# w_out handed over in chunk order, keys and bias in fewer loads, another order for the last pair's products, and seeded banks at the end

## The chip, the core and the metric

The kernel runs on one core of a Trainium2 chip. The core has a matmul engine (PE, with its weight loads shown as PEld), a vector engine (DVE), a scalar engine (ACT), GpSimd (POOL) and a queue engine (SP) that issues most of the DMAs; 16 DMA engines move the data. The metric is the device time of one execution in microseconds (us), the median of several runs.

## The reference

One trunk layer is run for two batches with the same weights: a prompt of 512 tokens and a sample of 1024 tokens, width 1024, in fp32. Attention has 8 heads of 64 in 2 key/value groups and sees a window of 128 to either side; beside it runs a convolution branch.

```python
h = rmsnorm(x, norm_attn_g)
z = h @ w_in                                   # q | k | v | ca | cb
a = window_attention(q, k, v, bias, sink)      # 512 columns
c = silu(layernorm(dwconv31(ca * sigmoid(cb)))) # 512 columns
x = x + concat(a, c) @ w_out
h = rmsnorm(x, norm_ffn_g)
u = dwconv3(h @ w_up)                          # 2 x 2816 columns
x = x + (silu(u[:, :2816]) * u[:, 2816:]) @ w_down
y = rmsnorm(x, norm_final_g)
```

## The kernel before, in words

Every fp32 operand is split into a high part (a cast to fp32r, ACT, L153) and a low part (the difference, DVE or POOL, L154), and each product is three passes on PE: high x high, high x low, low x high. A pass is a matmul of 128x128 by 128x512 that writes a PSUM bank of 128x512 fp32.

The stages are: the input projection of both batches, with the convolution branch and the attention of the prompt beside it (to about 283 us); the prompt's w_out product (about 288 to 345 us), beside which the attention of the sample begins; the prompt's feed-forward (to about 790 us) with the rest of the sample's attention beside it; the sample's w_out product (780 to 900 us); and the sample's feed-forward. There the up products are computed by a scheme of seven products in place of eight for each of 22 steps (`first` to `seventh`), the last of which is step 21, the last pair; the down products use the same scheme, product after product in the order 1, 2, 5, 6, 7, 4, 3, each over 11 pairs p, each on four token blocks tt (`mm_down`, L1468).

The parts that the change touches are these.

- **w_out of the prompt.** `prompt_out` walks two halves n of the 1024 output columns. `load_wo` (L746) loads the eight chunks kc of 128 rows; chunks 0 to 3 hold the attention's rows, whose two head groups lie apart in w_out, so each takes two loads of 64 rows (L753), and chunks 4 to 7 take one each (L755). `split_wo` splits them (L153, L154), and `out_half` runs the 24 matmuls of a token block (L727, L728, L729), then adds x on DVE.
- **Keys of the sample.** The projection wrote the split keys to a DRAM tensor `ksd` of 64 rows. `load_kv` (L759) loads them into four tiles of 128 rows x 1024, one for each of two head groups and of high and low (q9, q6, q7, q1 in the program's buffer numbers), with the same 64 rows in either half of the partitions: two loads of 64 rows a tile, 4096 B a row (L765). The score matmuls of the sample (`scores`, L583) read these tiles. `attention` of the sample is interleaved with `out_half`.
- **Bias.** `load_bias` (L508) loads the band bias of each head from a DRAM tensor `bbd`, one load a head (L513).
- **The last pair.** The loop over j calls the products by hand. In the last round the first down step (`down_step(0)`) stands between `seventh` and `fourth`. A product may need a value that another engine puts into its bank: `seventh` needs the copy of `sixth` (u2, L1243), `third` the sum that `y_sum` forms (L1266).
- **The end.** `finish` (L1525) forms the mean square of a row block from two halves, takes its power on POOL, scales on ACT and DVE and stores with SP. For the blocks 2 and 3, the last, the kernel first sums product 3 in a PSUM bank, adds it on DVE to the sum o12 (L1036), and squares that (L1530).

In the stretches around the change the order of the instructions on PE (in the feed-forward on PE and SP) is that in which the code is written, while the other engines, and PE outside those stretches, are ordered by a scheduler that simulates the program. SP's DMAs take turns on eight semaphores, so that at most eight are under way; the ninth waits for the first. Tiles come from a list of named slots (q, c, h, d, s for SBUF; a, u, b, c, w for PSUM); who takes a slot again waits until its last reader is done.

Of the kernel before, what the change touches and what calls it, by code (L numbers as in the profile page):

```python
# [9 lines left out]
F32 = mybir.dt.float32  # L10
# [89 lines left out]
def tile_hybrid_encoder(ctx: ExitStack, tc: tile.TileContext, xs, rel_bias, norm_attn_g, w_in,  # L100
# [70 lines left out]
    def want_w(i):  # L171
        if i < nch and i not in ws:
            want_raw(i)
            ws[i] = split(raws.pop(i))

    class Halves:
        def __init__(self, parts):
            self.parts = parts
# [567 lines left out]

    def load_wo(kc, n):
        raw = wor[kc, n] = sb.tile([NT])
        s = slice(n * NT, (n + 1) * NT)
        if kc < 4:  # L750
            for kv in range(NKV):
                r0 = (kv * GRP + kc) * HD
                nc.sync.dma_start(raw[kv * HD:(kv + 1) * HD, :], w_out[0, r0:r0 + HD, s])  # L753
        else:
            nc.sync.dma_start(raw[:], w_out[0, kc * P:(kc + 1) * P, s])  # L755

    def split_wo(kc, n, dve=False):
        wo[kc, n] = split(wor.pop((kc, n)), dve)

    def load_kv():  # L760
        for kv in range(NKV):
            kt[1, kv] = [sb.tile([1024], F32R) for _ in range(2)]
            for L in range(2):
                for half in range(2):
                    nc.sync.dma_start(kt[1, kv][L][half * HD:(half + 1) * HD, :].bitcast(F32), ksd[:, kv, L, :])  # L765
# [351 lines left out]
    class Part:  # L1117
        def __init__(self, held, n):
            self.held, self.n = held, n

        def __getitem__(self, i):
            return self.held[:, self.n, :][i]
# [98 lines left out]
    def pair_banks(j):  # L1221
        st[j] = dict(x=wide(), wy=wide())

    def armed(out):

        hi, lo = A[1, 0]
        nc.tensor.matmul(out, hi[:, 0:P], hi[:], start=True, stop=True)

    def first(j):
# [235 lines left out]
    LEAD = 4  # L1465
    CAP = 48

    def mm_down(out, i, p, tt):  # L1468
        (sh, sl), (th, tl) = hl[i, p]
        c = slice(tt * P, (tt + 1) * P)  # L1470
        nc.tensor.matmul(out, sh[:, c], th[:], start=(p == 0), stop=False)  # L1471
        nc.tensor.matmul(out, sh[:, c], tl[:], start=False, stop=False)  # L1472
        nc.tensor.matmul(out, sl[:, c], th[:], start=False, stop=(p == NPAIR - 1))  # L1473

    pair2 = lambda: [sb.tile([W2]) for _ in range(2)]
    xd = {}
# [38 lines left out]

    early = {}

    def left_first(tt):

        ss, o = early[tt] = sm(2), sb.tile([D])  # L1520
        part = cut(o11, tt)
        nc.scalar.activation(o[:, L], part, AF.Square, accum_out=ss[:, 0:1])
        nc.vector.tensor_tensor(part, part, fins[0][:, L], op=ALU.mult)

    def finish(blk, parts, tail):  # L1525
        ss, o = early.pop(blk) if tail else (sm(2), sb.tile([D]))
        rs = sm(2)
        for n in range(1 if tail else 0, 2):
            s = slice(n * NT, (n + 1) * NT)
            nc.scalar.activation(o[:, s], parts[n], AF.Square, accum_out=ss[:, n:n + 1])  # L1530
        nc.gpsimd.tensor_scalar(rs[:, 0:1], ss[:, 0:1], 1.0 / D, EPS, op0=ALU.mult, op1=ALU.add)
        nc.gpsimd.tensor_scalar(rs[:, 1:2], ss[:, 1:2], 1.0 / D, rs[:, 0:1], op0=ALU.mult, op1=ALU.add)  # L1532
        nc.gpsimd.tensor_tensor(rs[:, 1:2], rs[:, 1:2], nhalf[:, 0:1], op=ALU.pow)
        for n in range(2):
            s = slice(n * NT, (n + 1) * NT)
            if n == 0 and not tail:
                nc.scalar.activation(o[:, s], parts[n], AF.Identity, scale=rs[:, 1:2])
                nc.gpsimd.tensor_tensor(o[:, s], o[:, s], fins[0][:, s], op=ALU.mult)
            elif n == 0:
                nc.scalar.activation(o[:, s], parts[n], AF.Identity, scale=rs[:, 1:2])  # L1540
            else:
                nc.vector.scalar_tensor_tensor(o[:, s], parts[n], rs[:, 1:2], fins[0][:, s], op0=ALU.mult, op1=ALU.mult)  # L1542
            nc.sync.dma_start(GR[1]["o"][blk * P:(blk + 1) * P, s], o[:, s])

    made = 0

# [9 lines left out]
    def down_step(k):  # L1556
        i, p = steps[k]
        load_next(8 if k == 0 else 3 if len(pr) < CAP else 0)
        make(k + (LEAD if k else 1))
        if p == 0:  # L1560
            pd.extend(wide() for _ in range(2))
        for tt in range(4):
            mm_down(pd[tt // 2][:, (tt % 2) * NT:(tt % 2 + 1) * NT], i, p, tt)
        hl.pop((i, p))
        if p == NPAIR - 1:
            evacuate(i, pd)
            pd.clear()
# [12 lines left out]
        if i == 4 and p == 8:  # L1580
            with_x("o12", 0, 1)
            load_x1(1, 0)

    for j in range(2, NJ):
        for half in range(2):
            load_up(j + 3, half)
        if j >= NJ - 3:
            sb.free.extend(raws.free)
            raws.free.clear()
        if j >= NJ - 2:  # L1590
            load_next(4)
# [20 lines left out]
        third(j)  # L1612
        split_up(j + 1, 3)
    sb.free.extend(raws.free)
    value_part(NJ - 1)
# [4 lines left out]
    u, e, o11, o12 = (acc.pop(n) for n in ("u", "e", "o11", "o12"))  # L1620
    cut = lambda t, tt: t[tt // 2][:, (tt % 2) * NT:(tt % 2 + 1) * NT]
    base = len(steps) - NPAIR
    z = wide()
# [45 lines left out]

def _laid_out(np, v):  # L1670
    cols = lambda a: a.reshape(-1, P).T
    w_in = v["w_in"][0]
    cb, ca = (w_in[:, c:c + P].reshape(KC, P, P) for c in (COL_CB, COL_CA))
    laid = dict(
        xpT=v["x_prompt"][0].T.reshape(KC, P, NT),
        xsT=v["x_sample"][0].reshape(2, NT, KC, P).transpose(0, 2, 3, 1),
        w_in=_columns(w_in),
        w_up=_columns(v["w_up"][0]),
        w_first=np.concatenate([cb, ca], axis=2),
        vecs=np.concatenate([cols(v[n]) for n in ("norm_attn_g", "norm_ffn_g", "conv_dw_b", "conv_ln_g", "conv_ln_b", "ffn_dw_b")], axis=1),  # L1680
        cvw=cols(v["conv_dw_w"]),
        fw=cols(v["ffn_dw_w"]),
    )
    return {n: np.ascontiguousarray(a) for n, a in laid.items()}
# [27 lines left out]
```

## Time and profile before

| what | us |
|---|---|
| median of 3 runs | 1525.64 (1525.16 to 1525.9) |
| the profiled execution | 1529.8 |
| its span in the profile | 1528.0 |
| PE busy | 1492.7 (98% of the span) |
| DVE, ACT, POOL busy | 1177.5, 801.6, 742.9 |
| mean granted clock of PE | 0.995 |

A row of the list of waits names the engine, the tile and line that waited, whom it waited for, the us in total, how many times, and the longest. A row of the time line gives the start, the us, the engine, the line, the operation, the tiles (out<-in), and in brackets the idle time before it with what ended it. DMA rows on SPq show the issuing alone; the data land some us later, and the DMA view gives the median from issue to landing.

### The profile page before, as it was taken

The numbers are of one execution on the slowest core, as the hardware profiler recorded it, in microseconds if no ns is written. First come the engines' busy times: TensorE is split into PE (matmuls) and PEld (weight loads), VectorE is DVE, ScalarE is ACT, GpSimd is POOL, SyncE is SP. The second block draws the span as 40 slices with busy tenths as digits, with TensorE's granted clock in tenths as the row PEclk, the third lists the DMA queues.
The fourth block names the chain that finished last, engine by engine and source line by source line (L and its number), as shares of the span: only waits on it lengthen the run. The fifth ranks groups of instructions, "written<-read, shape, count | busy, mean of one in ns | idle before, by whom it ended". The sixth has DMA issues, their size and how long they took to land. (4 is left out here: it accounts for less than half of the span.)

```text
span 1528.0 us, 20034 instructions
## 1 busy us (share of the span) xinstructions
PE 1492.7 (98%) x6800; PEld 1226.7 (80%) x6800; DVE 1177.5 (77%) x1669; ACT 801.6 (52%) x1414; POOL 742.9 (49%) x648
## 2 busy tenths in 40 slices
PE   8999999899999999999999999999999999999997
PEld 7888777787888877878878888888888888788886
DVE  7877847558799989995575878888888877886794
ACT  6424454467566565665355365444444445454364
POOL 3454353228677777786542325555555554000236
PEclk9999999999999999999999999999999999999999
DMA  9455231834333333345474213333333323585642
GB/s 376 154 165 150 85 104 35 254 112 124 97 111 100 123 102 109 102 128 173 141 243 140 83 56 104 103 104 103 104 104 104 103 90 127 207 341 167 205 145 110
DMA packets 106754, 209.71 MB, mean 137 GB/s; under 512 B 11507, under 2 KB 31091, under 8 KB 106524
## 3 DMA queue, kind: packets, MB, share of 16 engines
q1 hardware_dynamic: 105404, 207.36, 41.0%
q8 instruction: 53, 0.87, 0.2%
q10 hardware_dynamic: 1248, 1.09, 0.2%
q14 instruction: 49, 0.40, 0.1%
HBM read 161.98 MB, written 47.46 MB: 137 GB/s over the span
## 5 line engine op out<-in xcount | busy, mean ns | idle before, releaser
L1039 POOL TENSOR_TENSOR q<-q,q 128x512 fp32r<-128x512 f32 x82 | 114.4, 1407 | 155.8 <-ACT q L1148 151.9
L154 POOL TENSOR_TENSOR q<-q,q 128x1024 fp32r<-128x1024 f32 x66 | 159.9, 2425 | 58.2 <-ACT q L153 21.2
L281 PE MATMUL u<-h,q 128*128 128x512 f32 x384 | 151.8, 395 | 1.3 <-DVE h L890 0.9
L282 PE MATMUL u<-h,q 128*128 128x512 f32 x384 | 150.5, 392 | 0.0
L283 PE MATMUL u<-h,q 128*128 128x512 f32 x384 | 150.2, 391 | 0.0
L1162 PE MATMUL w<-h,q 128*128 128x512 f32 x372 | 146.3, 393 | 2.4 <-ACT h L1243 1.5
L1164 PE MATMUL w<-h,q 128*128 128x512 f32 x372 | 144.9, 390 | 0.7 <-POOL q L1039 0.7
L322 DVE SCALAR_TENSOR_TENSOR c<-c,cvw,c 128x512 f32<-128x512 f32 x184 | 137.4, 747 | 1.7
L1163 PE MATMUL w<-h,q 128*128 128x512 f32 x350 | 136.3, 389 | 0.0
L1036 POOL TENSOR_TENSOR q<-q,q 128x1024 f32<-128x1024 f32 x8 | 23.9, 3001 | 180.8 <-DVE q L1036 169.4
L153 ACT CAST q<-q 128x1024 fp32r<-128x1024 f32 x66 | 69.1, 1050 | 67.6 <-POOL q L154 39.8
L1471 PE MATMUL w<-h,h 128*128 128x512 f32 x264 | 102.7, 389 | 0.0
L1473 PE MATMUL w<-h,h 128*128 128x512 f32 x264 | 102.7, 389 | 0.0
L1039 DVE TENSOR_TENSOR h<-h,h 128x512 fp32r<-128x512 f32 (+1 forms) x128 | 92.2, 762 | 11.1 <-ACT h L1043 9.0
L1039 POOL TENSOR_TENSOR c<-q,c 128x512 fp32r<-128x512 f32 x46 | 72.1, 1580 | 49.8 <-ACT c L1148 49.8
L1472 PE MATMUL w<-h,h 128*128 128x512 f32 x244 | 95.0, 390 | 0.0
L314 POOL TENSOR_TENSOR h<-h,h 128x512 f32<-128x512 f32 x57 | 76.1, 1335 | 28.4 <-ACT h L313 23.5
L1043 ACT CAST h<-h 128x512 fp32r<-128x512 f32 x101 | 58.7, 619 | 58.0 <-DVE h L1039 30.5
L1162 PEld LDWEIGHTS w<-h,q 128*128 128x128 f32 x372 | 69.8, 188 | 20.6 <-ACT w L1234 3.6
L281 PEld LDWEIGHTS u<-h,q 128*128 128x128 f32 x384 | 72.1, 188 | 16.9 <-DVE h L890 2.1
L154 POOL TENSOR_TENSOR h<-h,h 128x512 fp32r<-128x512 f32 x52 | 70.4, 1360 | 29.2 <-ACT h L153 19.7
L283 PEld LDWEIGHTS u<-h,q 128*128 128x128 f32 x384 | 72.1, 188 | 15.0 <-POOL q L154 0.4
(445 smaller groups left out, 4364.7 us busy)
## 6 DMA issues: line engine op xcount, KB each, us to landing
q<-in_laid_w_up SPq DMA_DIRECT2D x88, 512.0 KB, 3.6
h<-in_w_down SPq DMA_DIRECT2D x90, 256.0 KB, 3.6
ga<-q SPq DMA_DIRECT2D x64, 256.0 KB, 2.0
h<-ga SPq DMA_DIRECT2D x57, 256.0 KB, 3.9
q<-in_laid_w_in SPq DMA_DIRECT2D x22, 512.0 KB, 3.9
q<-in_x_sample SPq DMA_DIRECT2D x15, 512.0 KB, 6.0
h<-qsd SPq DMA_DIRECT2D x24, 256.0 KB, 3.3
qsd<-h SPq DMA_DIRECT2D x44, 128.0 KB, 2.4
```

The lines of the kernel that those rows point to most:

```text
L154: (nc.vector if dve else nc.gpsimd).tensor_tensor(lo[:], raw[:], hi[:].bitcast(F32), op=ALU.subtract)
L281: nc.tensor.matmul(out, whi[:, kc, :], hi[:], start=(kc == 0), stop=False)
L282: nc.tensor.matmul(out, whi[:, kc, :], lo[:], start=False, stop=False)
L283: nc.tensor.matmul(out, wlo[:, kc, :], hi[:], start=False, stop=(kc == KC - 1))
L322: nc.vector.scalar_tensor_tensor(acc[:], src(t), w(t), acc[:], op0=ALU.mult, op1=ALU.add)
L1039: (eng or nc.vector).tensor_tensor(out, a, b, op=ALU.subtract)
L1162: nc.tensor.matmul(out, whi[:, s], hi[:], start=(start and c == 0), stop=False, **go)
L1163: nc.tensor.matmul(out, whi[:, s], lo[:], start=False, stop=False, **go)
L1164: nc.tensor.matmul(out, wlo[:, s], hi[:], start=False, stop=(stop and c == 3), **go)
L1471: nc.tensor.matmul(out, sh[:, c], th[:], start=(p == 0), stop=False)
L1472: nc.tensor.matmul(out, sh[:, c], tl[:], start=False, stop=False)
L1473: nc.tensor.matmul(out, sl[:, c], th[:], start=False, stop=(p == NPAIR - 1))
```

## The change

w_out is handed over as a tensor in the order chunk by chunk, so that every chunk is one load of 128 rows. The two loads of a key tile become one, whose source repeats the 64 rows with a step of stride 0 in front. The bias loads of the heads that share a tile become one. In the last pair the call of `fourth` and `third` moves ahead of `seventh`, and `seventh` goes behind the first down step. At the end the banks for the last two blocks are armed and filled with o12 by ACT ahead of time, product 3 accumulates on top, and the square reads the bank; eps enters earlier, as a column of that bank, and the last block's two stores go out on ACT's and SP's queue.

```diff
     def load_bias(n):
...
-            for e in range(n):
-                nc.sync.dma_start(bt[:, e, :], bass.AP(b0.tensor, b0.offset + (h + e) * NT + P - 1, [[NH * NT - 1, P], [1, 3 * P]]))
-                bias.append((bt, e))
+            nc.sync.dma_start(bt[:], bass.AP(b0.tensor, b0.offset + h * NT + P - 1, [[NH * NT - 1, P], [NT, n], [1, 3 * P]]))
+            bias.extend((bt, e) for e in range(n))
...
     def load_wo(kc, n):
         raw = wor[kc, n] = sb.tile([NT])
-        s = slice(n * NT, (n + 1) * NT)
-        if kc < 4:
-            for kv in range(NKV):
-                r0 = (kv * GRP + kc) * HD
-                nc.sync.dma_start(raw[kv * HD:(kv + 1) * HD, :], w_out[0, r0:r0 + HD, s])
-        else:
-            nc.sync.dma_start(raw[:], w_out[0, kc * P:(kc + 1) * P, s])
+        nc.sync.dma_start(raw[:], laid["w_out"][n, :, kc, :])
...
             for L in range(2):
-                for half in range(2):
-                    nc.sync.dma_start(kt[1, kv][L][half * HD:(half + 1) * HD, :].bitcast(F32), ksd[:, kv, L, :])
+                k = ksd[:, kv, L, :]
+                nc.sync.dma_start(kt[1, kv][L][:].bitcast(F32), bass.AP(k.tensor, k.offset, [[0, 2]] + list(k.ap)))
...
-    def mm_down(out, i, p, tt):
+    def mm_down(out, i, p, tt, seeded=False):
...
-        nc.tensor.matmul(out, sh[:, c], th[:], start=(p == 0), stop=False)
+        go = dict(skip_group_check=seeded)
+        nc.tensor.matmul(out, sh[:, c], th[:], start=(p == 0 and not seeded), stop=False, **go)
...
+        if tail:
+            nc.scalar.activation(o[:, NT:D + 1], parts[2], AF.Square, accum_out=ss[:, 1:2])
+        else:
...
-        nc.gpsimd.tensor_scalar(rs[:, 0:1], ss[:, 0:1], 1.0 / D, EPS, op0=ALU.mult, op1=ALU.add)
-        nc.gpsimd.tensor_scalar(rs[:, 1:2], ss[:, 1:2], 1.0 / D, rs[:, 0:1], op0=ALU.mult, op1=ALU.add)
-        nc.gpsimd.tensor_tensor(rs[:, 1:2], rs[:, 1:2], nhalf[:, 0:1], op=ALU.pow)
...
+        nc.gpsimd.tensor_tensor(rs[:], ss[:, 1:2], nhalf[:, 0:1], op=ALU.pow)
...
-            nc.sync.dma_start(GR[1]["o"][blk * P:(blk + 1) * P, s], o[:, s])
+            (nc.scalar if n == 0 and tail else nc.sync).dma_start(GR[1]["o"][blk * P:(blk + 1) * P, s], o[:, s])
...
+            nc.scalar.activation(fins[0][:], fins[0][:], AF.Identity, scale=D ** 0.5)
...
+        last = j == NJ - 1
         value_part(j - 1)
+        if last:
+            fourth(j, None, True)
+            third(j)
         first(j + 1)
         split_up(j + 1, 6)
-        seventh(j)
-        if j == NJ - 1:
+        seventh(j, None, not last)
+        if last:
...
-        fourth(j)
+        if last:
+            y_sum(j)
+        else:
+            fourth(j)
...
+        if p == 4:
+            for tt in (2, 3):
+                zs.append(wide())
+                armed(zs[-1][:, L], hl[3, p][0][0])
+                nc.scalar.copy(zs[-1][:, L], cut(o12, tt))
...
     for tt in (2, 3):
-        left_first(tt)
-        z = wide()
+        z = zs.pop(0)
+        left_first(tt, z)
         for p in range(NPAIR):
-            mm_down(z[:, L], 3, p, tt)
-        add(cut(o12, tt), z[:, L], cut(o12, tt))
-        finish(tt, (cut(o11, tt), cut(o12, tt)), True)
+            mm_down(z[:, L], 3, p, tt, True)
+        finish(tt, (cut(o11, tt), z[:, L], z[:, 0:NT + 1]), True)
```

Line numbers shift by 7 to 27 in the changed kernel: the score matmuls are L589 there, w_out's L733 to L735, the products' L1164 to L1166, the down products' L1474 to L1476.

On SP, in the prompt's w_out product, this stood before (q6, q7 and q1 are key tiles; h58, h29, h57, h56 take w_out chunks and values; q0, q13, q2 rows of x):

```order
L769 DMA h29_438_2761<-vsd_156 128x512
L755 DMA h57_492_3031<-in_w_out 128x512
L755 DMA h56_493_3033<-in_w_out 128x512
L765 DMA q6_432_2745<-ksd_157 64x1024 x2
L765 DMA q7_433_2750<-ksd_157 64x1024 x2
L765 DMA q1_434_2751<-ksd_157 64x1024 x2
L142 DMA q0_472_2883<-in_x_prompt 128x1024
L142 DMA q13_478_2927<-in_x_prompt 128x1024
L142 DMA q2_482_2979<-in_x_prompt 128x1024
L753 DMA h18_487_3018<-in_w_out 64x512 x2
L753 DMA h6_481_2976<-in_w_out 64x512 x2
```

And this stands there now:

```order
L755 DMA h56_493_3017<-in_laid_w_out 128x512
L778 DMA h29_438_2753<-vsd_156 128x512
L774 DMA q6_432_2741<-ksd_157 128x1x1024
L774 DMA q7_433_2744<-ksd_157 128x1x1024
L774 DMA q1_434_2745<-ksd_157 128x1x1024
L142 DMA q0_472_2871<-in_x_prompt 128x1024
L142 DMA q13_478_2915<-in_x_prompt 128x1024
L755 DMA h18_487_3005<-in_laid_w_out 128x512
L142 DMA q2_482_2966<-in_x_prompt 128x1024
L755 DMA h6_481_2964<-in_laid_w_out 128x512
```

Six key loads of 64 rows became three of 128, at the same place, ahead of the same rows of x and the last two chunks of w_out. The fourth key tile, q9, is loaded ahead of all the w_out chunks, before as now.

On PE, at the end of the second token block's w_out product (bank u1) and the start of the third's (u0), the score matmuls of the sample stood so before (banks a0, a1, a2):

```order
L727 MATMUL u1_134_2929<-h12_467_2830,h34_407_2575 128x512
L728 MATMUL u1_134_2929<-h11_468_2831,h34_407_2575 128x512
L729 MATMUL u1_134_2929<-h12_467_2830,h16_408_2576 128x512
L583 MATMUL a0_130_2861<-q9_431_2744,h39_459_2808 128x256
L583 MATMUL a0_130_2861<-q6_432_2745,h39_459_2808 128x256
L583 MATMUL a1_132_2908<-q7_433_2750,h0_460_2810 128x256
L583 MATMUL a1_132_2908<-q1_434_2751,h0_460_2810 128x256
L583 MATMUL a2_133_2914<-q7_433_2750,h0_460_2810 128x256
L583 MATMUL a2_133_2914<-q1_434_2751,h0_460_2810 128x256
L727 MATMUL u0_137_2981<-h52_447_2784,h17_396_2505 128x512
```

And so now:

```order
L733 MATMUL u1_134_2917<-h12_467_2818,h34_407_2571 128x512
L734 MATMUL u1_134_2917<-h11_468_2819,h34_407_2571 128x512
L589 MATMUL a0_130_2849<-q9_431_2740,h39_459_2796 128x256
L589 MATMUL a0_130_2849<-q6_432_2741,h39_459_2796 128x256
L589 MATMUL a1_132_2896<-q7_433_2744,h0_460_2798 128x256
L589 MATMUL a1_132_2896<-q1_434_2745,h0_460_2798 128x256
L735 MATMUL u1_134_2917<-h12_467_2818,h16_408_2572 128x512
L733 MATMUL u0_137_2968<-h52_447_2772,h17_396_2501 128x512
L734 MATMUL u0_137_2968<-h51_448_2773,h17_396_2501 128x512
L589 MATMUL a2_133_2902<-q7_433_2744,h0_460_2798 128x256
L589 MATMUL a2_133_2902<-q1_434_2745,h0_460_2798 128x256
```

The first score matmuls on q7 and q1 stand one matmul earlier, ahead of the last pass of the second block.

On PE, in the last pair, behind `sixth` (bank w_44, right operand q_1756) came the first down step (w_45) and then `seventh` (q_1758), before:

```order
L1164 MATMUL w_44_11786<-h_1441_8783,q_1756_11800 128x512
L1471 MATMUL w_45_11975<-h_1783_11963,h_1781_11959 128x512
L1472 MATMUL w_45_11975<-h_1784_11964,h_1781_11959 128x512
L1473 MATMUL w_45_11975<-h_1783_11963,h_1782_11960 128x512
L1471 MATMUL w_45_11975<-h_1783_11963,h_1781_11959 128x512
L1472 MATMUL w_45_11975<-h_1784_11964,h_1781_11959 128x512
L1473 MATMUL w_45_11975<-h_1783_11963,h_1782_11960 128x512
L1162 MATMUL w_44_11786<-h_1443_8795,q_1758_11831 128x512
```

Now `fourth` (w_43, q_1761) follows `sixth` at once, and `seventh` stands between two passes of the fifth down step:

```order
L1166 MATMUL w_44_11762<-h_1441_8759,q_1756_11776 128x512
L1164 MATMUL w_43_11761<-h_1427_8684,q_1761_11828 128x512
L1165 MATMUL w_43_11761<-h_1428_8685,q_1761_11828 128x512
L1166 MATMUL w_43_11761<-h_1427_8684,q_1761_11828 128x512
L1164 MATMUL w_43_11761<-h_1429_8696,q_1761_11828 128x512
```

```order
L1474 MATMUL w_45_11977<-h_1807_12041,h_1805_12037 128x512
L1475 MATMUL w_45_11977<-h_1808_12042,h_1805_12037 128x512
L1164 MATMUL w_44_11762<-h_1443_8771,q_1758_11807 128x512
L1165 MATMUL w_44_11762<-h_1444_8772,q_1758_11807 128x512
L1166 MATMUL w_44_11762<-h_1443_8771,q_1758_11807 128x512
```

`third` stands between, behind the first half of the first down step.

More of the change, by code (lines that the diff above doesn't have):

```diff
@@ L174, in want_w, with __init__, __getitem__ @@
             ws[i] = split(raws.pop(i))
+    class Part:
+        def __init__(self, held, n):
+            self.held, self.n = held, n
+        def __getitem__(self, i):
+            return self.held[:, self.n, :][i]
     class Halves:
@@ L748, in load_wo, with load_wo_pair @@
         raw = wor[kc, n] = sb.tile([NT])
-        s = slice(n * NT, (n + 1) * NT)
-        if kc < 4:
-            for kv in range(NKV):
-                r0 = (kv * GRP + kc) * HD
-                nc.sync.dma_start(raw[kv * HD:(kv + 1) * HD, :], w_out[0, r0:r0 + HD, s])
-        else:
-            nc.sync.dma_start(raw[:], w_out[0, kc * P:(kc + 1) * P, s])
+        nc.sync.dma_start(raw[:], laid["w_out"][n, :, kc, :])
+    def load_wo_pair(kc, n):
+        both = sb.tile([2, NT])
+        nc.sync.dma_start(both[:], laid["w_out"][n, :, kc:kc + 2, :])
+        for m in range(2):
+            wor[kc + m, n] = Part(both, m)
     def split_wo(kc, n, dve=False):
-        wo[kc, n] = split(wor.pop((kc, n)), dve)
+        raw = wor.pop((kc, n))
+        hi, lo = wo[kc, n] = sb.tile([NT], F32R), sb.tile([NT], F32R)
+        nc.scalar.copy(hi[:], raw[:])
+        (nc.vector if dve else nc.gpsimd).tensor_tensor(lo[:], raw[:], hi[:].bitcast(F32), op=ALU.subtract)
     def load_kv():
@@ L1222, in pair_banks, with armed @@
         st[j] = dict(x=wide(), wy=wide())
-    def armed(out):
-        hi, lo = A[1, 0]
+    def armed(out, hi=None):
+        hi = hi or A[1, 0][0]
         nc.tensor.matmul(out, hi[:, 0:P], hi[:], start=True, stop=True)
@@ L1516, in tile_hybrid_encoder, with squares, left_first @@
     early = {}
-    def left_first(tt):
-        ss, o = early[tt] = sm(2), sb.tile([D])
+    def squares(ss, n, part, o):
+        nc.scalar.activation(o, part, AF.Square, accum_out=ss[:, n:n + 1])
+        if n == 0:
+            nc.gpsimd.tensor_scalar(ss[:, 0:1], ss[:, 0:1], 1.0, D * EPS, op0=ALU.mult, op1=ALU.add)
+    def left_first(tt, z):
+        ss, o = early[tt] = sm(2), sb.tile([D + 4])
         part = cut(o11, tt)
-        nc.scalar.activation(o[:, L], part, AF.Square, accum_out=ss[:, 0:1])
+        squares(ss, 0, part, o[:, L])
+        nc.gpsimd.tensor_tensor(ss[:, 0:1], ss[:, 0:1], half[:], op=ALU.pow)
+        nc.scalar.copy(z[:, NT:NT + 1], ss[:, 0:1])
         nc.vector.tensor_tensor(part, part, fins[0][:, L], op=ALU.mult)
@@ L1526, in finish @@
         ss, o = early.pop(blk) if tail else (sm(2), sb.tile([D]))
[L1527 to L1543 removed]
+        rs = sm(1)
+        if tail:
+            nc.scalar.activation(o[:, NT:D + 1], parts[2], AF.Square, accum_out=ss[:, 1:2])
+        else:
+            for n in range(2):
+                squares(ss, n, parts[n], o[:, n * NT:(n + 1) * NT])
+            nc.gpsimd.tensor_tensor(ss[:, 1:2], ss[:, 1:2], ss[:, 0:1], op=ALU.add)
+        nc.gpsimd.tensor_tensor(rs[:], ss[:, 1:2], nhalf[:, 0:1], op=ALU.pow)
+        for n in (1, 0):
+            s = slice(n * NT, (n + 1) * NT)
+            if n == 0:
+                nc.scalar.activation(o[:, s], parts[n], AF.Identity, scale=rs[:])
+                if not tail:
+                    nc.gpsimd.tensor_tensor(o[:, s], o[:, s], fins[0][:, s], op=ALU.mult)
+            else:
+                nc.vector.scalar_tensor_tensor(o[:, s], parts[n], rs[:], fins[0][:, s], op0=ALU.mult, op1=ALU.mult)
+            (nc.scalar if n == 0 and tail else nc.sync).dma_start(GR[1]["o"][blk * P:(blk + 1) * P, s], o[:, s])
     made = 0
@@ L1608, in tile_hybrid_encoder @@
         split_up(j + 1, 7)
-        fourth(j)
+        if last:
+            y_sum(j)
+        else:
+            fourth(j)
         gate_part(j)
         split_up(j + 1, 4)
-        third(j)
+        if not last:
+            third(j)
         split_up(j + 1, 3)
@@ L1622, in tile_hybrid_encoder @@
     base = len(steps) - NPAIR
+    zs, half = [], sm(1)
+    nc.gpsimd.memset(half[:], 0.5)
     z = wide()
@@ L1671, in _laid_out @@
     cols = lambda a: a.reshape(-1, P).T
-    w_in = v["w_in"][0]
+    w_in, w_out = v["w_in"][0], v["w_out"][0]
     cb, ca = (w_in[:, c:c + P].reshape(KC, P, P) for c in (COL_CB, COL_CA))
```

11 lines of the change are left out of this document (4 added, 7 removed).

## The prediction

> **What bounds the kernel now.** I read the page's busy times first, then the list of waits of PE (the matmul engine), then the table of windows around the longest wait, and last the time line of the places that the change touches. The first row of the page is engine by engine the busy time, its share of the span and the instructions:
>
> ```profile
> PE 1492.7 (98%) x6800; PEld 1226.7 (80%) x6800; DVE 1177.5 (77%) x1669; ACT 801.6 (52%) x1414; POOL 742.9 (49%) x648
> ```
>
> PE is busy for 98% of the span and takes its instructions strictly in order, so time is won where PE waits or at the end behind PE, and lost where a new wait is put in front of it. Its waits, longest first (total us, times, longest):
>
> ```profile
> PE u L727 <- DVE q L628: 5.3, 1, 5.3
> ...
> PE a L240 <- DVE h L628: 2.3, 1, 2.3
> ...
> PE w L1162 <- ACT h L1243: 1.5, 1, 1.5
> ...
> PE w L1162 <- DVE w L1036: 0.6, 1, 0.6
> ```
>
> Around the longest wait the table of windows (window, sum of us, then busy us of PE, PEld, DVE, ACT, POOL, granted clock, DMA share, GB/s) shows a second cost:
>
> ```profile
> 284.00:288.00 4.00, 0.00 (x0) 0.00 (x0) 2.23 (x5) 1.72 (x4) 3.30 (x3) 0.87 1.01 309
> 288.00:292.00 4.00, 3.46 (x8) 2.81 (x9) 4.00 (x9) 3.73 (x9) 0.00 (x0) 0.50 1.05 308
> 292.00:296.00 4.00, 4.00 (x15) 3.15 (x14) 2.06 (x4) 0.62 (x1) 1.08 (x2) 0.77 0.81 246
> ```
>
> PE stands until 288.5, and then works with half the clock: 3.46 us at 0.50 and 4 us at 0.77 lose 1.73 + 0.92 = 2.6 us on top of the 5.3. The Trainium skill ("TensorE: Matmul & The Clock Gate", Part 1 on the clock gate) says that an idle window of about 3.4 us halves the clock until a busy window has passed; these rows agree, and by it a restart after a long wait costs 1.7 to 3.4 us.
>
> **The key loads, the term that decides.** The keys of the sample batch (tile names q from ksd) were read in pairs of 64-row loads, one for each half of the partitions. Now each is one load whose source steps twice with stride 0 over the same 64 rows, while its destination has 128 rows. The question is how many of the 16 DMA engines share such a load. The trace shows it for row counts: the DMA view of 65 to 67 us holds one write of 8 rows, that of 268 to 272 us one pair of 64-row loads:
>
> ```profile
> DMA packets 16, 0.02 MB, mean 8 GB/s; under 512 B 8, under 2 KB 8, under 8 KB 16
> ...
> bvd<-h SPq DMA_DIRECT2D x1, 16.0 KB
> ```
>
> ```profile
> DMA packets 160, 0.52 MB, mean 131 GB/s; under 512 B 32, under 2 KB 32, under 8 KB 160
> ...
> q1 hardware_dynamic: 160, 0.52, 45.5%
> ...
> q<-ksd SPq DMA_DIRECT2D x2, 256.0 KB, 3.8
> ```
>
> Beside the data packets there are tiny ones (under 512 B): 8 for the transfer of 8 rows, 32 for two transfers of 64 rows, 16 each. I read them as one end mark from each engine that took part: a transfer is cut along its outermost step, and a step of 8 gets 8 engines. The new load has 2 as the outermost step of its source, and cutting both sides alike leaves two engines. That the source's step counts, and not only the destination's 128 rows, no row shows; it is my choice, and the first rival is its opposite. The Trainium skill ("DMA: Bandwidth & Descriptors", section "Why a DMA increments its semaphore by 16 and not by 1") gives this as a rule: the largest number up to 16 that divides the slowest step longer than one of both sides. The counts above agree; no run here shows a transfer with unlike sides.
>
> Price of one load on two engines. Where all 16 are kept busy, the windows show what they move together:
>
> ```profile
> 10.00:14.00 4.00, 4.00 (x11) 3.08 (x10) 4.00 (x4) 4.00 (x8) 4.00 (x3) 1.00 1.04 417
> ...
> 30.00:34.00 4.00, 4.00 (x20) 3.30 (x19) 4.00 (x8) 4.00 (x7) 0.04 (x1) 1.00 1.02 416
> ```
>
> 417 GB/s are 52.1 for two engines, and 128 x 4096 B = 0.524 MB take 10.1 us. From above: the pair at 268 us held 45.5% of 16 engines for 4 us, 29.1 engine-us, so 14.6 us on two. The second has the cold start of both halves in it and the first is a steady rate; a load of 64 packets an engine is nearer to the steady one, and I take 10.1.
>
> Where it falls: SP (the DMA queue) issues one of these loads at 268 us ahead of the w_out loads, and three in a row from 292.8 (start, us, line, count):
>
> ```profile
> 268.15 1.14 SPq L765 DMA_DIRECT2D q<-ksd  x2
> 272.40 1.29 SPq L755 DMA_DIRECT2D h<-in_w_out  x3
> 273.78 5.52 SPq L753 DMA_DIRECT2D h<-in_w_out  x8
> ...
> 292.79 5.49 SPq L765 DMA_DIRECT2D q<-ksd  x6
> ```
>
> and PE multiplies them in the score matmuls (L583), six of them at 309.5:
>
> ```profile
> 305.55 0.52 PE L583 MATMUL a<-q,h 128*128 128x256 f32 x3
> ...
> 309.54 0.88 PE L583 MATMUL a<-q,h 128*128 128x256 f32 x6
> ```
>
> As the section on the change shows, the three loads stay back to back, and the fourth of the score matmuls at 309.5 now reads the last of them, q1. From issue to landing a 256 KB half took 3.8 us in the quiet window, of which 0.6 is moving at 417 GB/s, so 3.2 are fixed. The last key load lands at 292.8 + 3.2 + 3 x 10.1 = 326.3 where PE wants it at 309.9: 16.4 us of wait, in one piece of about 6 us (second load) and one of 10. Behind a wait of 10 us I set the clock loss of the row above, 2.6 (0 to 4). While PE stands, DVE, ACT and POOL catch up, so that waits behind it shrink (the 2.3 at L240 is the next): I take 1.0 back. **Sum +18.0.** Nothing hides it: PE has no other instruction that may go first, and the busy engines here are two of sixteen, so the loads can't be hurried. Queued behind the three on the same two engines are x_prompt, the last w_out chunks and the bias; their shares follow within some 5 us, about when PE has come to them.
>
> **w_out.** The same bytes in chunk order. Four chunks that took eight half loads (the 5.52 us row) take four of some 0.43 us. But the first key load is now ahead of them on two engines until about 268.2 + 3.2 + 10.1 = 281.5, so the chunk that ACT needs first lands some 2 us later than now, not earlier, and the 5.3 us wait stays or grows. It costs nothing beside the 16.4, which ends at a landing and not at PE's pace: 0. The bias loads (eight to four) and the w_out loads of the sample batch lie far from PE's waits: 0, some 1 us at worst.
>
> **The last pair.** PE now does fourth and third ahead of seventh, which goes behind most of the first down products. That takes away the two waits of 1.5 and 0.6 at L1162, 2.1 us. A new one can come where the second down product begins (1339.2 now): in the new order ACT copies the first product's bank (L1492) ahead of the cast for it.
>
> ```profile
> 1336.67 0.62 ACT L1043 CAST h<-q 128x512 fp32r<-128x512 f32 x1 [0.43 <-PE w L1473]
> ...
> 1338.03 1.02 ACT L1492 COPY q<-w 128x1024 f32<-128x1024 f32 x1 [0.73 <-PE w L1473]
> ...
> 1339.19 0.39 PE L1471 MATMUL w<-h,h 128*128 128x512 f32 x1
> ...
> 1340.95 0.69 DVE L1039 TENSOR_TENSOR h<-q,h 128x512 fp32r<-128x512 f32 x1 [2.94 <-ACT h L1043]
> ```
>
> From the copy's start at 1338.03 the copy, the cast and DVE's low half are 1.02 + 0.62 + 0.69 = 2.33, to 1340.4, against PE's 1339.2 + some 0.3 that the next matmul can wait: 0.9 (0 to 1.3). **Sum -1.1** (-2.1 to +0.2).
>
> **The end.** Now, behind PE's last matmul (start, us):
>
> ```profile
> 1518.02 7.18 SPq L1543 DMA_DIRECT2D out_sample<-q  x7
> ...
> 1518.75 0.39 PE L1473 MATMUL w<-h,h 128*128 128x512 f32 x1
> ...
> 1521.17 0.68 DVE L1036 TENSOR_TENSOR q<-w,q 128x512 f32<-128x512 f32 x1
> 1521.89 0.63 ACT L1530 ACTIVATE q<-q 128x512 f32<-128x512 f32 x1 [0.67 <-DVE q L1036]
> 1522.43 0.19 ACT L1530 ACTIVATION_READ_ACCUMULATOR q<-q 128x1 f32 x1
> 1522.71 0.27 POOL L1532 TENSOR_SCALAR s<-s,s 128x1 f32<-128x1 f32 x1 [2.24 <-ACT q L1530]
> 1523.06 0.55 POOL L1533 TENSOR_TENSOR s<-s,nhalf 128x1 f32<-128x1 f32 x1
> ...
> 1523.65 0.75 DVE L1542 SCALAR_TENSOR_TENSOR q<-q,s,q 128x512 f32<-128x512 f32 x1 [1.79 <-POOL s L1533]
> ```
>
> With seeded banks the add at 1521.17 goes, and the square starts when PE ends, at 1519.14 instead of 1521.89: -2.75. The POOL step from 1522.71 to 1523.06 goes too: -0.35. DVE's last result is there at 1524.40, and SP has issued both stores by 1525.20, so on two queues one issue of 0.4 goes. Two arming matmuls come in on PE, which gives a 128x512 matmul some 0.23: +0.45. **Sum -3.05**, which I round to -3.0 (-2.0 to -3.3; a square that reads PSUM need not be dearer, since the 128x1024 copy above takes 1.02 from PSUM). The extra scaling of the final gain on ACT, one pass of 128x1024, lies under PE: 0.
>
> Together +18.0 - 1.1 - 3.0 = +13.9. The profiled execution took 1529.8 us (span 1528.0, and 1.8 around it); the median of the runs is 1525.64, 4.2 below it. So 1525.64 + 13.9 = **1539.5 us** for the median.
>
> **The rivals.** (1) The new key loads are cut along their 128 destination rows and use 16 engines as before. Then the front part pays: the first cast's chunk arrives some 3 us earlier, of an upper bound of 5.3 + 2.6 = 7.9 that would need the whole wait gone. For it: the destination has 128 rows, as in the loads that reached 417 GB/s. Against it: 8 rows got 8 marks, so the number of steps does bind, and the source has to be cut too. Time: 1525.64 - 3.0 - 1.1 - 3.0 = 1518.5 (1514 to 1523), faster. It decides from the point where three loads fit into 309.9 - 296.0 = 13.9 us, 4.6 each, 113 GB/s or some 4.4 engines. Chance 0.19. (2) Sixteen engines, but the front wait stays because the chain behind the first cast (ACT, DVE, POOL, DVE) is crowded anyway, and the last pair's later value chain delays operands by what it saves: 1523 to 1528. Chance 0.03. (3) Two engines and the price of the cold row: 3 x 14.6, 13.5 us more, 1553, slower still; it is the upper end of my own case. That case has 0.78.
>
> **How the numbers follow.** Forecast 1539.5; its own range is 1534 (no clock loss, more caught up) to 1553. It holds about nine tenths of 0.78, so to leave out no more than 2 in 10 the range goes down to 1519, into the first rival. A measurement can tell about 0.2%, 3 us, from no change. Faster: rival 1, 0.19. Same: 0.04 (rival 2 and edges). Slower: 0.77.
>
> **What would show it.** In the changed profile: two tiny packets for each key load; from about 295 to 326 us a DMA share near 0.12 with some 50 GB/s in the table of windows; a wait of PE at the score matmuls of 10 us or more that ends with q1's landing, then half the clock; L1162's two waits gone; the square within 0.5 us of PE's end. Wrong I am if key loads have 16 marks, if the score matmuls don't wait, or if the three loads land within 10 us.

## The result, and the profile after

The changed kernel takes 1550.33 us (median of 5 runs, 1548.05 to 1552.44) against 1525.64 (1525.01 to 1526.8) of the kernel before on the same chip: 1.0163 times as long, 95% interval 1.0148 to 1.0178, 24.7 us. The forecast was 1539.5 with a range of 1519 to 1553: slower by the mechanism that was named, with its price too small. The profiled execution took 1549.82 us with a span of 1548.0, that is 20.0 above the span before.

The list of waits of PE in the changed kernel (total us, times, longest) has a new first row, and the rows around it changed:

```profile
PE a L589 <- DMA q<-ksd: 16.6, 3, 10.2
PE a L709 <- DVE h L703: 4.4, 2, 4.3
PE u L733 <- DVE q L634: 4.2, 1, 4.2
```

The score matmuls wait for the key loads, three times. The time line of PE shows the three stops, each released by a load:

```profile
310.46 1.22 PE L589 MATMUL a<-q,h 128*128 128x256 f32 x4 [2.36 <-DMA q<-ksd]
...
321.35 0.55 PE L589 MATMUL a<-q,h 128*128 128x256 f32 x1 [3.98 <-DMA q<-ksd]
...
332.12 0.58 PE L589 MATMUL a<-q,h 128*128 128x256 f32 x1 [10.22 <-DMA q<-ksd]
```

The releases are 10.89 and 10.77 us apart. That it is two engines stands in the DMA view of 302 to 312 us, in the midst of the three loads:

```profile
DMA packets 132, 0.53 MB, mean 53 GB/s; under 512 B 2, under 2 KB 2, under 8 KB 132
...
q1 hardware_dynamic: 132, 0.53, 12.9%
```

0.53 MB in 10 us, 12.9% of 16 engines (two are 12.5%), and two end marks, those of one load. So the load ran on two engines, though its destination has 128 rows; that this is due to the two outer steps of the source and not to the repeated rows, the experiments show. The rule of the Trainium skill that I named ("DMA: Bandwidth & Descriptors", section "Why a DMA increments its semaphore by 16 and not by 1") holds here for unlike sides too, which no trace of before showed.

The table of windows has the two prices one behind the other, a PE that stands and then a PE with half its clock (us of PE, PEld, DVE, ACT, POOL; clock, DMA share, GB/s):

```profile
300.00:304.00 4.00, 4.00 (x22) 3.38 (x21) 1.39 (x2) 2.61 (x6) 0.80 (x2) 1.00 0.12 50
304.00:308.00 4.00, 4.00 (x19) 3.08 (x17) 1.39 (x2) 1.30 (x3) 0.86 (x2) 1.00 0.13 53
308.00:312.00 4.00, 1.64 (x7) 1.45 (x7) 0.90 (x4) 0.39 (x1) 0.00 (x0) 0.76 0.13 53
...
324.00:328.00 4.00, 0.00 (x0) 0.00 (x0) 0.00 (x0) 0.00 (x0) 0.00 (x0) 0.50 0.43 132
328.00:332.00 4.00, 0.00 (x0) 0.00 (x0) 0.00 (x0) 0.00 (x0) 0.00 (x0) 0.50 0.13 52
332.00:336.00 4.00, 2.94 (x8) 2.15 (x9) 1.67 (x6) 1.22 (x3) 0.00 (x0) 0.50 0.15 56
```

At 324 to 332 us not one engine computes: DVE, ACT and POOL have run dry behind PE. The DMA share of 0.13 is what a reader should stop at: the loads are slow while fourteen engines rest.

Following the same instructions through both traces gives the account. At 282 us of before, ahead of w_out, the changed kernel is 0.3 us late. Its first w_out pass is 4.5 us late (293.07 against 288.54), as the chunks come late and PE stands twice, 4.3 and 4.2 us. The score matmul that waits for q1 is 22.2 us late (332.12 against 309.89); this end is set by the landing and not by the 4.5. Where the order of the passes is again the same in both, at 315.7, it is 25.7. At 346.7 it is 26.4; up to the last pair 2.6 of that is caught up, so 23.8 remain. The last pair takes 1.5 back (22.3 at ACT's copy behind the second down product, 1420.14 against 1397.87). PE's last matmul is 22.6 late (1541.39 against 1518.75), and behind it 2.6 are won, so that 20.0 remain.

Of the 3.5 us between 22.2 and 25.7, 0.2 is a w_out pass that stood ahead of the q1 matmul before and stands behind it now. A further 0.9 is a wait that the forecast did not have: DVE's add behind the second token block waits for rows of x, whose load came in behind the key loads, and PE waits for the add:

```profile
333.32 0.69 DVE L738 TENSOR_TENSOR q<-u,q 128x512 f32<-128x512 f32 x1 [21.34 <-DMA q<-in_x_prompt]
```

```profile
334.06 0.80 PE L733 MATMUL u<-h,h 128*128 128x512 f32 x1 [0.94 <-DVE q L738]
```

The other 2.3 are half clock: from 332.1 to 337.5 us most passes start 0.43 us apart instead of 0.23.

The end, in the order of the instructions behind PE's last matmul:

```profile
1541.39 0.39 PE L1476 MATMUL w<-h,h 128*128 128x512 f32 x1
1541.82 0.60 ACT L1539 ACTIVATE c<-w 128x513 f32<-128x513 f32 x1 [4.92 <-PE w L1476]
1542.31 0.19 ACT L1539 ACTIVATION_READ_ACCUMULATOR c<-w 128x1 f32 x1
1542.58 0.55 POOL L1544 TENSOR_TENSOR s<-s,nhalf 128x1 f32<-128x1 f32 x1 [6.45 <-ACT c L1539]
1543.16 0.72 ACT L1548 ACTIVATE c<-q,s 128x512 f32<-128x512 f32 x1 [0.66 <-POOL s L1544]
```

The square starts 0.04 us after PE's end at 1541.78. From there to the end of the span it is 6.2 us, before it was 8.9 (1528.0 less 1519.14).

### The profile page after: what moved, and what is told of

Read it like the earlier page. It is cut to its first block, busy times and chain, and to the rows that moved or that the text cites. A ratio compares the mean times of both kernels' runs of the same rounds, so it can differ in the third digit from the quotient of the medians.

```text
span 1548.0 us, 19996 instructions
## 1 busy us (share of the span) xinstructions
PE 1498.2 (97%) x6802; PEld 1230.9 (80%) x6802; DVE 1171.0 (76%) x1668; ACT 803.0 (52%) x1419; POOL 744.7 (48%) x649
## 5 line engine op out<-in xcount | busy, mean ns | idle before, releaser
L1048 POOL TENSOR_TENSOR q<-q,q 128x512 fp32r<-128x512 f32 x82 | 117.6, 1445 | 156.2 <-ACT q L1150 150.5
L1164 PE MATMUL w<-h,q 128*128 128x512 f32 x372 | 145.7, 392 | 0.3 <-ACT w L1236 0.3
L1166 PE MATMUL w<-h,q 128*128 128x512 f32 x372 | 144.9, 390 | 0.7 <-POOL q L1048 0.7
L1474 PE MATMUL w<-h,h 128*128 128x512 f32 x264 | 102.8, 390 | 0.4 <-ACT h L1052 0.4
L1476 PE MATMUL w<-h,h 128*128 128x512 f32 x264 | 102.7, 389 | 0.0
L288 PEld LDWEIGHTS u<-h,q 128*128 128x128 f32 x384 | 72.2, 188 | 16.6 <-DVE h L899 2.1
L602 ACT ACTIVATE h<-h,s 128x385 f32<-128x385 f32 (+1 forms) x95 | 55.1, 580 | 58.5 <-DVE s L593 56.7
L290 PEld LDWEIGHTS u<-h,q 128*128 128x128 f32 x384 | 72.1, 188 | 15.0 <-POOL q L154 0.4
L289 PEld LDWEIGHTS u<-h,q 128*128 128x128 f32 x384 | 72.2, 188 | 13.8
```

The lines of the kernel that those rows point to most:

```text
L288: nc.tensor.matmul(out, whi[:, kc, :], hi[:], start=(kc == 0), stop=False)
L289: nc.tensor.matmul(out, whi[:, kc, :], lo[:], start=False, stop=False)
L290: nc.tensor.matmul(out, wlo[:, kc, :], hi[:], start=False, stop=(kc == KC - 1))
L1048: (eng or nc.vector).tensor_tensor(out, a, b, op=ALU.subtract)
L1164: nc.tensor.matmul(out, whi[:, s], hi[:], start=(start and c == 0), stop=False, **go)
L1166: nc.tensor.matmul(out, wlo[:, s], hi[:], start=False, stop=(stop and c == 3), **go)
```

## The experiments

Each run is set against the kernel before on its own chip, where the medians of before lay between 1526.62 and 1527.74. Two runs are therefore compared by their ratios; one part in a thousand is 1.5 us.

**Key loads back in pairs.**

```diff
-                k = ksd[:, kv, L, :]
-                nc.sync.dma_start(kt[1, kv][L][:].bitcast(F32), bass.AP(k.tensor, k.offset, [[0, 2]] + list(k.ap)))
+                for half in range(2):
+                    nc.sync.dma_start(kt[1, kv][L][half * HD:(half + 1) * HD, :].bitcast(F32), ksd[:, kv, L, :])
```

> The changed kernel with the key loads back in pairs of 64 rows; everything else of the change stays. Theory (a key load in one runs on 2 of 16 engines, and that alone makes the loss): no wait of PE for the keys, 16 end marks for each load, and the rest of the change shows: 1518 to 1522 us, 4 to 7 below the kernel before. Rival (the rest of the change loses too, by w_out's new order or the last pair's): 1526 us or more.

Measured: 1521.98 us against 1526.62, ratio 0.9971 (0.9960 to 0.9981), at the upper end of the forecast. The wait for the keys is gone from the list of waits of PE, whose first rows are:

```profile
PE u L733 <- DVE q L634: 4.4, 1, 4.4
PE u L469 <- ACT h L435: 2.5, 1, 2.5
```

So the one expression costs some 29 us (1.0163 less 0.9971), and without it the rest of the change is 4.4 us faster than the kernel before (2.9 to 6.1). This version beats both kernels.

**Key loads in one, and nothing else of the change.** The same edit, the other way, in the kernel before.

> The kernel before with the key loads in one and nothing else of the change. Theory: 2 engines for each load, some 10.8 us each as in the changed kernel, PE waits 15 us or more at the score matmuls; 1546 to 1554 us. Rival (the loss comes from the key loads together with w_out's new order): below 1535.

Measured: 1554.99 us, ratio 1.0184 (1.0168 to 1.0200), 1 us above the forecast. The loss needs nothing else of the change. The DMA view of 303 to 313 us has the same two marks, and PE's stop is one of 18.5 us:

```profile
DMA packets 132, 0.53 MB, mean 53 GB/s; under 512 B 2, under 2 KB 2, under 8 KB 132
```

```profile
334.26 1.20 PE L583 MATMUL a<-q,h 128*128 128x256 f32 x4 [18.53 <-issue]
```

"issue" is what the profile writes where it has found no releaser. The wait at w_out, 5.3 us before, is 10.7 here.

**Two steps without repetition.** The keys are written twice, with a gap row between, so that the outer step has a real stride.

```diff
-    ksd = dr.tile([HD, NKV, 2, 1024], F32, name="ksd")
+    ksd = dr.tile([2 * (HD + 1), NKV, 2, 1024], F32, name="ksd")
...
-                nc.sync.dma_start(kt[1, kv][L][:].bitcast(F32), bass.AP(k.tensor, k.offset, [[0, 2]] + list(k.ap)))
+                row = k.ap[0][0]
+                nc.sync.dma_start(kt[1, kv][L][:].bitcast(F32),
+                                  bass.AP(k.tensor, k.offset, [[(HD + 1) * row, 2], [row, HD], [1, 1024]]))
```

> The changed kernel with the keys written twice to DRAM, 128 rows with a gap row in the middle, and each key load in one with 2 outer steps of a real stride: nothing is read twice. Theory (the count of the outermost step sets the engines): 2 end marks, 10 to 11 us for each load, 1547 to 1553 us as the changed kernel. Rival (reading the same rows twice at once is slow): 16 engines' speed, 1518 to 1523 us.

Measured: 1555.14 us, ratio 1.0183 (1.0166 to 1.0200), 2 us above the forecast, with two marks and the same 53 GB/s in the DMA view of 306 to 316 us:

```profile
DMA packets 131, 0.53 MB, mean 53 GB/s; under 512 B 2, under 2 KB 2, under 8 KB 131
```

Nothing is read twice here, and it is as slow. Reading the same rows twice is not the cause; the two steps are.

**Eight steps, with gap rows.**

Here `row` is the distance of two key rows in DRAM.

```diff
+                            nc.sync.dma_start(bass.AP(k.tensor, k.offset, [[17 * row, 4], [row, 16], [1, NT]]), src_k)
...
+                                  bass.AP(k.tensor, k.offset, [[17 * row, 8], [row, 16], [1, 1024]]))
```

> The same, with 8 outer steps of 16 rows and gap rows between them, in one load a tile. Theory: 8 engines, 8 end marks, 0.524 MB at half of 417 GB/s in 2.5 us a load, all three within 8 us of the first issue, no wait or up to 2 us at the score matmuls: 1518 to 1524 us. Rival (a load of 128 rows in one is late by its size or its many steps): 1530 us or more.

Measured: 1538.91 us, ratio 1.0080 (1.0063 to 1.0097): a miss of 15 us. PE's first waits name the reason, and it is not the key loads:

```profile
PE b L402 <- DVE h L399: 4.9, 1, 4.9
PE u L736 <- DVE q L637: 3.9, 1, 3.9
PE u L649 <- DVE h L637: 2.6, 1, 2.6
```

At 155 us of before this trace is already 11.3 us behind, when the keys are being written. To have gaps, I had made each write of 64 rows end in 4 outer steps. The DMA view of 152 to 160 us shows these writes:

```profile
DMA packets 382, 0.80 MB, mean 100 GB/s; under 512 B 25, under 2 KB 25, under 8 KB 382
...
q1 hardware_dynamic: 382, 0.80, 26.1%
```

100 GB/s and 26% of 16 engines: four engines for four steps, on the writing side. My experiment had the fault that it was to measure, in another place. What eight steps do on the reading side, this run does not tell.

**128 plain rows, one load.** The keys are written twice without a gap, by writes of 64 rows as before.

```diff
+                nc.sync.dma_start(kt[1, kv][L][:].bitcast(F32), ksd[:, kv, L, :])
```

> The changed kernel with the keys written twice to DRAM as 128 plain rows, and each key load in one of 128 rows: one outermost step count of 128 on both sides. Theory: 16 end marks, no wait of PE for keys; half as many key issues as in pairs for eight writes more: within 2 us of the changed kernel with pairs, 1518 to 1523 us. Rival (one 512 KB load in place of two is what is slow): 1530 us or more.

Measured: 1525.64 us, ratio 0.9989 (0.9978 to 1.0000), and 16 marks in the DMA view of 269 to 274.5 us:

```profile
DMA packets 144, 0.52 MB, mean 95 GB/s; under 512 B 16, under 2 KB 16, under 8 KB 144
```

One load of 512 KB is not slow as such. By the ratios the run lies 2.7 us above the pairs, and it missed its forecast by 2.6. Its trace falls 2.0 us behind that of the pairs around 155 to 225 us, where the eight extra writes are, but is level again at w_out's first pass; what makes the 2.7 stays open.

**Eight steps on the same plain rows.** Only the reading differs from the run before. The key rows reach the tile in another order, so that the sample's scores come from permuted keys.

```diff
+                nc.sync.dma_start(kt[1, kv][L][:].bitcast(F32), bass.AP(k.tensor, k.offset, [[row, 8], [8 * row, 16], [1, 1024]]))
```

> The kernel with 128 plain key rows in DRAM, whose writes are as in the run e3, but read with 8 outer steps of one row and 16 inner steps of eight rows; the rows then reach the tile in another order, so the sample's scores are computed from permuted keys. Theory: 8 end marks and about 200 GB/s for each load, 2.5 us, no wait at the score matmuls, the time of e3 (1525.6) within 3 us. Rival (8 steps cost as in e5, 12 us, by the reading): 1534 us or more.

Measured: 1531.29 us, ratio 1.0022 (1.0011 to 1.0033), by the ratios 5.0 above the plain rows, and between both forecasts. The DMA view of 270.5 to 276.4 us holds one load, with eight marks, and PE does wait once:

```profile
DMA packets 147, 0.55 MB, mean 93 GB/s; under 512 B 8, under 2 KB 8, under 8 KB 147
```

```profile
310.18 0.39 PE L590 MATMUL a<-q,h 128*128 128x256 f32 x1 [2.81 <-DMA q<-ksd]
```

```profile
300.00:304.00 4.00, 4.00 (x22) 3.35 (x21) 1.59 (x5) 1.14 (x5) 0.00 (x0) 1.00 1.04 225
304.00:308.00 4.00, 3.37 (x17) 2.66 (x15) 0.00 (x0) 0.00 (x0) 0.00 (x0) 1.00 0.94 208
```

My mistake was to price the loads as if they were alone. They are issued at 292.6 into a queue that already holds w_out's and v's loads, and 208 GB/s is then the speed of all that stands before and behind them. Why engines that are busy for 0.94 of the time moved half of the 417 GB/s here, no run settles. Behind the wait PE waits another 1.1 us for DVE and then has half the clock. Marks of 2, 8 and 16 (the changed kernel, this run, the run before) go with waits for the keys of 16.6, 2.8 and 0 us.

**Only the first key load as a pair.** The three others stay in one.

```diff
+                if kv == 0 and L == 0:
+                    for half in range(2):
+                        nc.sync.dma_start(kt[1, kv][L][half * HD:(half + 1) * HD, :].bitcast(F32), k)
+                else:
```

> The changed kernel with the first key load (ahead of the w_out loads) as a pair of 64-row loads, the other three in one. Theory (the first load on 2 engines only delays SP and the three behind, as the wait at the scores ends at the last landing): the three are issued at 292 us instead of 297, the last lands near 327 instead of 332, 1545 to 1547 us, 4 to 5 below the changed kernel's 1550. Rival (the three set their own time, the first costs nothing, as my prediction had it): 1549 to 1551.

Measured: 1545.54 us, ratio 1.0119 (1.0102 to 1.0135), below the changed kernel by 4.8 us in the medians and by 6.7 in the ratios. SP issues the three at 291.50, and PE goes on at 326.62:

```profile
291.50 9.00 SPq L778 DMA_DIRECT2D q<-ksd  x3
```

```profile
326.62 0.58 PE L589 MATMUL a<-q,h 128*128 128x256 f32 x1 [11.17 <-DMA q<-ksd]
```

In the changed kernel these were 297.15 and 332.12, 5.7 and 5.5 us later. The path leads over SP. Of its DMAs the ninth waits for the first, and counted from the first key load the ninth is the eighth w_out load. SP's list of waits in the changed kernel has this one, and the row of the eight issues is 9.98 us long there and 3.66 here:

```profile
SPq L755 <- DMA q<-ksd: 6.2, 1, 6.2
```

```profile
272.67 9.98 SPq L755 DMA_DIRECT2D h<-in_laid_w_out  x8
```

```profile
272.81 3.66 SPq L755 DMA_DIRECT2D h<-in_laid_w_out  x8
```

My forecast had put the first load at 0.

**Only the first key load in one.** The mirror image (`if kv or L` above).

> The changed kernel with only the first key load in one, the other three as pairs. Theory: no wait at the scores; the w_out chunks land some 5 us later than in the pairs kernel, PE's waits ahead of w_out sum to 8 us instead of 4 to 5 and half-clock windows come with them: 1526 to 1531 us against the pairs kernel's 1522. Rival (one load on 2 engines is hidden): 1521 to 1523.

Measured: 1529.13 us, ratio 1.0016 (1.0005 to 1.0028), by the ratios 6.9 above the pairs. There is no wait for keys, but the chunks of w_out come late:

```profile
PE a L709 <- DVE h L703: 5.6, 2, 5.2
PE u L733 <- DVE q L634: 4.2, 1, 4.2
```

The two experiments price the two parts of the loss, by the ratios: 6.9 us for the first load alone, 22.6 for the other three alone, 29.3 for all four. Within the intervals, of some 2 us to either side, they add up.

**The last pair and the end alone; w_out's order alone.** The kernel before with these parts of the diff as they stand, and nothing else.

```diff
+        if last:
+            fourth(j, None, True)
+            third(j)
...
+            mm_down(z[:, L], 3, p, tt, True)
```

> The kernel before with the last pair's order and the seeded banks alone; w_out, keys and bias loaded as before. By the trace of the changed kernel these parts give 1.9 and 2.1 us: 1521 to 1522.5 us. Rival (they were hidden by the long wait and cost or gain nothing by themselves): 1525 to 1526.

```diff
+        nc.sync.dma_start(raw[:], laid["w_out"][n, :, kc, :])
```

> The kernel before with w_out in chunk order, one load a chunk, alone. My term for it with the key loads unharmed was 3.0 us less (0.5 to 6): 1522 to 1525 us, the wait at w_out's first matmul 2 to 4 us instead of 5.3. Rival (the chain behind the first cast is crowded anyway): 1525 to 1527 with that wait still above 5.

Measured: 1525.41 (0.9988, 0.9979 to 0.9996) and 1525.29 (0.9990, 0.9981 to 0.9999) against 1527.17. Each gains, by 1.8 and 1.5 us (0.6 to 3.2, and 0.2 to 2.9); together 3.3, within the interval of what the pairs kernel shows. The bias loads were not run alone. Both times missed their forecasts, the first by 2.9 us and the second by 0.3, though in the second the wait at w_out's first matmul fell to 2.4 us as the theory had it. Both gains are smaller than a single trace says: the trace of w_out's order alone has a span of 1520.2, 7.8 below the trace of before, while its median is 1.9 below.

**An add on DVE instead of POOL.** From ACT's first cast of a w_out chunk on (279.59 and 277.89 us) the traces of the pairs kernel and of that with w_out alone keep step for 2.7 us. Then they part at one instruction, ahead of PE's wait at w_out, which is 4.4 us in the one and 2.4 in the other:

```profile
282.32 4.04 POOL L657 TENSOR_TENSOR q<-q,q 64x512 fp32r<-64x512 f32 x1 [4.33 <-DVE q L655]
```

```profile
280.62 1.75 POOL L651 TENSOR_TENSOR q<-q,q 64x512 fp32r<-64x512 f32 x1 [2.99 <-DVE q L649]
```

```diff
-        nc.gpsimd.tensor_tensor(cat[1][rows, :, :].rearrange("p j t -> p (j t)"), d[rows, :], c[rows, :], op=ALU.add)
+        (nc.vector if i == 3 and kv == 0 else nc.gpsimd).tensor_tensor(cat[1][rows, :, :].rearrange("p j t -> p (j t)"), d[rows, :], c[rows, :], op=ALU.add)
```

> The changed kernel with the key loads in pairs, and the add of the prompt's seventh attention unit (L657) on DVE instead of POOL. In the trace of the pairs kernel that add took 4.04 us on POOL beside a row of DVE splits, in that of w_out alone 1.75, and PE's wait at w_out was 4.4 and 2.4 us. Theory (POOL's add, held up by DVE's splits, sets the end of that wait): the wait falls to 3.5 us or less in every trace, with one half-clock window less at best; 1518 to 1521 us, 1 to 3 below the pairs kernel's 1522. Rival (the chain behind it is as long on DVE): 1521 to 1523, the wait above 4.

Measured: 1522.58 us, ratio 0.9971 (0.9960 to 0.9981), the same ratio as the pairs kernel. In its trace the wait is down to 2.7 us, as the theory had it, but the time is that of the rival, and the medians can't tell the two kernels apart:

```profile
PE u L733 <- DVE q L634: 2.7, 1, 2.7
```

So in these traces the add sets the end of that wait, and what it is worth over many executions is not shown to be above nothing; the interval of 0.1% to either side is 1.6 us.

## Why the prediction was right, and where its size was off

- **Two engines for a key load**: right. Two marks, 53 GB/s, 12.9% of 16 engines; with 8 steps 8 marks, with 128 rows 16, and two steps without repetition as slow as the change. The choice that carried 0.78 of the chance was the right one.
- **10.1 us a load**: near. The first of the three releases PE 13.3 us behind its issue (297.15 to 310.46), which is the forecast's 3.2 + 10.1. The two others follow 10.9 and 10.8 apart, 1.5 us more over both, although 53 GB/s would move 0.524 MB in 9.9 us; what takes the rest is not shown.
- **Where it falls, "292.8 + 3.2 + 3 x 10.1 = 326.3"**: the start was wrong. It was 297.15, and PE went on at 332.1: 4.4 us of the 5.8 are the start, 1.5 the two later loads. The step that failed is "It costs nothing beside the 16.4", on the first key load: that the wait ends at a landing is true, but the landing itself hangs on SP. SP waited 6.2 us for the first key load, then for the late chunks, before it could issue the three. The run with the first load as a pair puts that at 4.8 to 6.7 us (5.5 in the trace). I had listed what stood behind the load on the DMA engines, and not what stood behind it on SP. The chunk that ACT needs first came 4.4 us late (284.80 against 280.38) instead of 2, and the wait at w_out became two of 4.3 and 4.2.
- **Clock, +2.6**: 2.3 over the restart. The rows of x "about when PE has come to them" were 0.9 late and had been put at nothing. **Caught up, 1.0**: 2.6.
- **The last pair, -1.1**: 1.5 in the trace (23.8 to 22.3 late). The forecast's own terms, 2.1 gone and 0.9 new, give -1.2, and their bounds -2.1 to -0.8. Both waits at the products are gone. The new wait where the second down product begins is 0.4 + 0.2; by the starts of the passes (1360.06 to 1361.88) it costs 1.1, inside the 0.9 (0 to 1.3) that I gave it:

```profile
PE w L1474 <- ACT h L1052: 0.4, 1, 0.4
...
PE w L1475 <- DVE h L1048: 0.2, 1, 0.2
```

- **The end, -3.0**: 2.6 behind PE's last matmul; ahead of it PE loses 0.4 (22.3 to 22.6), about the two arming matmuls. That makes 2.3.
- **From the span to the median**: the trace accounts for +20.0, the medians differ by 24.7. I set the forecast off against a profiled execution that lay 4.2 above its own median, as if the same excess would be in the other; the changed kernel's profiled execution lies 0.5 below its median. Which instruction makes one execution of a kernel some us longer than another is not settled; 29 executions of the kernel before on one chip spread from 1524.24 to 1531.28.
- **The range**: that 1550.33 lies inside it is partly luck. Its upper end, 1553, was rival 3's price of 14.6 us a load, and a load took 10.8 to 10.9; the late start and the profiled execution's excess filled the gap.
- **Rival 1** (sixteen engines, 1518.5) is the time of a kernel that could be run, the pairs: 1522.0. Its mechanism for the front, an earlier first chunk, is there (277.89 in the trace of w_out alone, 280.38 before), and 3.0 us for it was twice what was measured (1.5, 0.2 to 2.9). The later parts alone gained 1.8 and not the 4.1 that I had put.

## What to carry to other kernels

Before two loads are merged into one, write down the outermost step of both sides: a small count there, as a repetition with stride 0 in front, was the number of DMA engines in these runs (2, 4 and 8). Here the merged load released PE 13.3 us behind its issue, where one of 128 plain rows landed in 3.8, though it is one instruction less. A wait that hides an earlier delay does so only if its own end doesn't hang on that delay; follow the queue that issues, not only the engines that move. And a sum made against one profiled execution is only as good as that execution: set its time beside the median first, and size gains below a few us on medians.

## What the runs showed of the hardware that was not expected

- The issue instruction itself can stand. SP's two loads of x behind the three key loads took 17 us to issue, while the DMA share stood near 0.13, two of 16 engines. What held the instruction, the trace does not name:

```profile
301.42 17.04 SPq L142 DMA_DIRECT2D q<-in_x_prompt  x2
```

- The cut holds for writes too: four outer steps at the DRAM side gave 100 GB/s and 26.1% of 16 engines.
- The length of a wait does not tell the clock behind it. Behind the wait of 2.36 us in the changed kernel, at 310.46, the next passes took 0.63 us; behind one of 2.40 in w_out alone they took 0.39 to 0.47.
- A POOL add of 64x512 took 4.04 us while DVE ran five splits in 3.1 us, and 1.75 while the same five took 4.2: which of the two gave way differed between the pairs kernel and that with w_out alone, one trace each, and with it the wait of PE by 2 us and a half-clock window.
